# Attention's last reciprocals behind the projection's first split, its first tile by blocks of channels, and late ranks in layer 1

## The chip, the cores and the metric

The kernel runs on one core of a Trainium2 chip. The metric is device microseconds (us) of one execution. The kernel before takes 2798.72 us, the median of three runs (2797.06 to 2804.81).

## The reference

Two layers of a diffusion transformer block over 1024 latent tokens and 256 context tokens, 1024 channels wide. In each layer the normed tokens go through one input projection into four mixers of 256 channels each (a gated linear recurrence, a chunked gated recurrence, a state-space scan and latent attention with four heads); their outputs are concatenated, projected, gated and added, and an expert layer follows in which each of 16 experts picks its tokens.

```
h = modulate(rmsnorm(x, norm1_w[l]), mod_l[0], mod_l[1])
...
p = softmax(scores); y_m = p @ v                      # attention: latents see context and latents
x = x + mod_l[2] * (concatenate([ya, yb, ys, ym]) @ w_out[l])
h = modulate(rmsnorm(x, norm2_w[l]), mod_l[3], mod_l[4])
x = x + mod_l[5] * expert_choice_ffn(h, moe_router[l], ...)
# the context goes the same way in layer 0; layer 1 drops it after the mixers
```

The change concerns the end of attention (`ym`) and the start of `concatenate(...) @ w_out`.

## The kernel before, in words

Work is written as generators ("threads": `mla` for attention, `lw` for w_out, `wout` and `woutc` for the projection of latents and context, `route`, `exp` and others), each with a rank in `ORDER`, a low number first. `weave` (line 230) takes the ready thread of the lowest rank, lets it emit instructions up to its next `yield`, and advances a planner's clock. A `yield "s"` leaves a thread ready at once, a yield of a number makes it wait that long on the planner's clock, `wait` and `room` yield False until a flag is set or a pool of buffers has room. What comes out is an order by priority; a compiler's scheduler then fills each engine's queue from it, by priority among what it takes to be ready, and each engine works through its queue in that order. `issue_after(ins)` tells that scheduler that an instruction stands behind `ins` on its engine.

Products in float32 are made of three float32r products: every operand is split into a high half (copied by ScalarE) and a low half (subtracted by VectorE) (`split`, line 537); a "block" of one channel group is three matmuls of 128x512.

Attention (`attend`, line 1440) works on a pair of heads and two halves of 512 latents. For each of ten groups of keys it makes scores (three matmuls for each of four combinations of half and head), exponentials on ScalarE (into C tiles E in the first pass, M tiles in the others), products with the values, and running sums of the exponentials in E. At the end a matmul with ones gives the sums, VectorE takes their reciprocal and multiplies. Pair 0's result is stored in the DRAM tensor yT (line 1484); pair 1's stays in SBUF as y7, high and low.

`load_wout` (line 1498) loads w_out in eight pieces of 128 channels, splits them, and sets the flags `w{l}.0` to `w{l}.7`; pieces 0 to 4 may be split when pair 0's scores are done, 5 to 7 when pair 1's are, for they take over attention's buffers (tag A). `wout` (line 1525) goes over tiles of 128 tokens: two for the context (layer 0 only, first) and eight for the latents. A tile is loaded from yT (line 1542) and split; its two halves of 512 output channels take eight blocks of three matmuls each; VectorE gates and adds, ScalarE squares, VectorE norms and modulates, POOL adds, and TensorE transposes the tile for the router. The context's tiles have all eight channel groups in yT; the latents' take groups 0 to 6 from yT and group 7 from y7. The next tile's loads and split are emitted one tile ahead, in the first tile only behind its last block (`load(1)`). In layer 1 `wout` starts at rank 2.5, and goes back to rank 30 when its first loads are emitted.

Of the kernel before, what the change touches and what calls it, by code (L numbers as in the profile page):

```python
# [9 lines left out]
F32 = mybir.dt.float32  # L10
# [11 lines left out]
D = 1024  # L22
# [18 lines left out]
    dict(derived=0.5, ada0=-2, ada=20, norm=-3, eproj=1, lru0=6.01, lru1=8.078, gate0=3.4, gate1=7.01, ssd=3.43, z=6.95,  # L41
         g=7, v=0.079, hgrn0=6.614, hgrn1=6.757, group0=1.91, group1=3.41, hout0=6.767, hout1=3.44, chunk=6.713, prep=1.5,
         mla=6.757, max=3.4, lw=3.41, wout=30, route=31, woutc=29, routec=31.5, exp=33, al=0.74, be=0.25, be_g=0.14,
         be_hgrn0=1.01, be_lw=1.45, al_hout1=1.15, be_chunk=0.09, al_eproj=0.65, al_max=1.21, al_lru0=0.43, al_g=0.92,
         be_lru0=1.2, al_group1=0.69, be_hout0=1.85, al_hgrn0=1.12, be_gate1=0.49, be_mla=0.48, **{
# [120 lines left out]
class Model:  # L166
# [51 lines left out]
    def wait(self, *names):  # L218
        while not all(n in self.done for n in names):
            yield False  # L220

    def rank(self, name, p):
        for th in self.threads:
            if th[4] == name:
                th[0] = p

    def spawn(self, l, key, g, more=0.0):
        self.threads.append([self.order[l][key] + more, len(self.threads), 0.0, g, f"{key}{l}", key, None])
# [308 lines left out]
    def split(self, w, tag, tag2=None):  # L537

        nc = self.nc
        hi = self.t(tag, list(w.shape), F32R)  # L540
        lo = self.t(tag2 or tag, list(w.shape), F32R)
        nc.scalar.activation(hi, w, AF.Copy)
        nc.vector.tensor_sub(lo, w, hi.bitcast(F32))
        return hi, lo

    def proj_ch(self, l, c0, evac, groups=GROUPS):
# [769 lines left out]
    def mla(self, l, need):  # L1316
        nc = self.nc
        c, idx, _, _ = self.cols[l]
        c0 = 0 if need else 2
        SCALE = 96.0 ** -0.5  # L1320
        yield from self.wait(f"prep{l}")
        while self.left[l]:
            yield False
        vd = self.vd
        qs = self.t("qs", [128, 1])
        nc.vector.memset(qs, SCALE)
        nc.vector.scalar_tensor_tensor(qs[0:64], c[0:64, idx["qn"]:idx["qn"] + 1], SCALE,
                                       c[0:64, idx["kn"]:idx["kn"] + 1], op0=ALU.mult, op1=ALU.mult)

        HI = [self.t("A", [128, 2, 2, NT], F32R) for _ in range(2)]  # L1330
        LO = [self.t("A", [128, 2, 2, NT], F32R) for _ in range(2)]
        onef = self.ones[96:97, 0:1]
        for i in range(2):
            nc.gpsimd.memset(LO[i][96:97].rearrange("p a h t -> p (a h t)").bitcast(F32), 0.0)
            nc.scalar.activation(HI[i][96:97, 1].rearrange("p h t -> p (h t)"), onef.to_broadcast([1, 2 * NT]), AF.Copy)
        lat = [(256, 512), (768, 512)]
        runs = [(pr, [(0, 256)], 2) for pr in range(2) if need] + [(pr, lat, CH) for pr in range(2)]

        def maxima():
            for i, (pr, parts, ns) in enumerate(runs):  # L1340
                yield from self.att_max(l, HI[pr], parts, ns)
                self.done.add(f"max{l}.{i}")
        self.spawn(l, "max", maxima())
        X = {}

        def load(t, q):
            X[t, q] = self.t("M", [128, 4, 96])
            nc.sync.dma_start(X[t, q].rearrange("p h e -> p (h e)"), self.qkd[q, 128 * t:128 * t + 128, :])

        def place(t, q):  # L1350
            x = X.pop((t, q))
            T = slice(128 * t, 128 * t + 128)
            pk = self.p([128, 4, 128])
            for h in range(4):
                nc.tensor.transpose(pk[0:96, h, :], x[:, h, :], self.ident)
            for i in range(2):
                ph = pk[0:96, 2 * i:2 * i + 2]
                hi, lo = HI[i][0:96, 1 - q, :, T], LO[i][0:96, 1 - q, :, T]
                if q:
                    nc.scalar.activation(hi, ph, AF.Copy, scale=qs[0:96])  # L1360
                    nc.vector.scalar_tensor_tensor(lo, ph, qs[0:96], hi.bitcast(F32), op0=ALU.mult, op1=ALU.subtract)
                else:
                    nc.scalar.activation(hi, ph, AF.Copy)
                    nc.vector.tensor_sub(lo, ph, hi.bitcast(F32))
        todo = [(t, 0) for t in range(CH)] + [(t, 1) for t in range(c0, CH)]
        for x in todo[:2]:
            load(*x)
        yield 3.0
        for i, x in enumerate(todo):
            if i + 2 < len(todo):  # L1370
                load(*todo[i + 2])
            place(*x)
            self.done.add(f"qk{l}.{x[0]}.{x[1]}")
            yield 0.0
        yield from self.room(4)
        V = [self.t("C", [128, CH // 2, 256]) for _ in range(2)]
        for i in range(2):
            nc.sync.dma_start(V[i], vd[640 * i:640 * i + 640, :].rearrange("(c p) e -> p c e", p=128))
        for i, (pr, parts, ns) in enumerate(runs):
            yield from self.wait(f"max{l}.{i}")  # L1380
            keep = None
            if ns == CH and pr == 1:
                yield from self.room(2)
                keep = self.y7 = [self.t("C", [128, NL], F32R) for _ in range(2)]
            yield from self.attend(HI[pr], LO[pr], V, pr, parts, ns, keep, f"att{l}.{pr}" if ns == CH else f"attc{l}.{pr}")
            if ns == CH:
                self.done.add(f"pair{l}.{pr}")
        self.free(4)
# [48 lines left out]
                nc.scalar.activation(HI[96:97, 0, hh, t0:t0 + n], pr_[96:97, :n], AF.Copy)  # L1437
            yield True

    def attend(self, HI, LO, V, pr, parts, ns, keep, flag):  # L1440
        nc = self.nc
        py = [self.p() for _ in parts]
        E = [self.t("C", [128, 2, 512]) for _ in parts]
# [29 lines left out]
            yield "s"  # L1473
        self.done.add(flag)

        for pi, (t0, n) in enumerate(parts):
            ps = self.p()
            for hh in range(2):
                nc.tensor.matmul(ps[64 * hh:64 * hh + 64, :n], self.ones[:, 0:64], E[pi][:, hh, :n], start=True, stop=True)
            o = self.t("M", [128, 512])  # L1480
            nc.vector.reciprocal(o[:, :n], ps[:, :n])
            nc.vector.tensor_mul(o[:, :n], o[:, :n], py[pi][:, :n])
            if keep is None:
                nc.scalar.dma_start(self.yT[768 + 128 * pr:896 + 128 * pr, t0:t0 + n], o[:, :n])
            else:
                hi, lo = [y[:, t0 - NC_:t0 - NC_ + n] for y in keep]
                nc.scalar.activation(hi, o[:, :n], AF.Copy)
                nc.vector.tensor_sub(lo, o[:, :n], hi.bitcast(F32))
            yield "s"
        yield "s"  # L1490

    def bcast_mod(self, l, s, j, tag="C"):

# [31 lines left out]
    def wout(self, l, s, base, h2d, logits):  # L1525
# [20 lines left out]
            Y[j] = hl, x  # L1546

        load(0)
        G = self.bcast_mod(l, s, 2)
        self.rank(f"wout{'c' if s else ''}{l}", 29 if s else 30)  # L1550
        yield 4.0

        def body(j):
# [1 line left out]
            xm = X[j] = self.t("W", [128, D])  # L1555
            ss = self.t("s1", [128, 2])
            pms = [self.p() for _ in range(2)]
            todo = [(hf, k) for hf in range(2) for k in range(own)] + [(hf, k) for hf in range(2) for k in range(own, 8)]
            if j:
                todo.sort()  # L1560
            for hf, k in todo:
                c = slice(512 * hf, 512 * hf + 512)
                pm = pms[hf]
                if True:
                    if k < own:
                        yh, yl = [y[:, k, :] for y in hl]
                    else:
                        yield from self.wait(f"pair{l}.1")
                        yh, yl = [y[:, 128 * j:128 * j + 128] for y in self.y7]
                    yield from self.wait(f"w{l}.{k}")  # L1570
                    w, wl = self.whi[k], self.wlo[k]
                    for pas, (y, w) in enumerate(((yh, w), (yl, w), (yh, wl))):
                        nc.tensor.matmul(pm, y, w[:, c], start=(k == 0 and pas == 0), stop=(k == 7 and pas == 2))
                    if k in (2, 4, 6):
                        yield "s"
                if k < 7:
                    continue
                if hf and j == 0:
                    yield from self.room(4)
                    n2 = self.t("C", [128, D])  # L1580
                    nc.sync.dma_start(n2, a["norm2_w"][l:l + 1].to_broadcast([128, D]))
                    A2 = self.bcast_mod(l, s, 4)
                    nc.vector.scalar_tensor_tensor(A2, A2, 1.0, n2, op0=ALU.add, op1=ALU.mult)
                    B2 = self.bcast_mod(l, s, 3)
                    mods.extend((A2, B2))
                    load(1)
                nc.vector.tensor_mul(xm[:, c], pm, G[:, c])
                nc.vector.tensor_add(x[:, c], x[:, c], xm[:, c])
                nc.scalar.activation(xm[:, c], x[:, c], AF.Square, accum_out=ss[:, hf:hf + 1])
# [496 lines left out]
    def layer(self, l):  # L2086
# [14 lines left out]
        if "o" in self.which:  # L2101
# [7 lines left out]
            if need:  # L2109
                lgc = self.t("lgc", [128, 2, 16])  # L2110
                self.spawn(l, "woutc", self.wout(l, 1, basec, h2c, lgc))
                self.spawn(l, "routec", self.route(l, 1, lgc, 2, 32))
            if not need:

                self.rank(f"wout{l}", 2.5)
            self.spawn(l, "exp", self.experts(l, need, base, basec, h2d, h2c))
        self.weave(l)
        if "o" in self.which:
# [54 lines left out]
```

## Time and profile before

| | |
|---|---|
| median of three runs | 2798.72 us |
| profiled execution | 2805.27 us, span 2803.2 us |
| TensorE matmul / weight load | 2422.1 us (86%) / 1847.7 us (66%) |
| VectorE / ScalarE / POOL | 1837.3 us (66%) / 1179.8 us (42%) / 766.5 us (27%) |
| share of the chain that ended last | PE 18%, DVE 7% are the largest |

The span is the time from the first to the last instruction of one profiled execution, and the share of an engine is its busy time in it. An engine's idle time is given in brackets in the timeline, with what ended it. Line 162 is a helper through which all computing instructions go, so instructions are told apart by the tags of their tiles (A, C, W, M; ps is PSUM, cf the identity, wr the router, sT the modulation's vector).

### The profile page before, as it was taken

The numbers are of one execution on the slowest core, as the hardware profiler recorded it, in microseconds if no ns is written. First come the engines' busy times: TensorE is split into PE (matmuls) and PEld (weight loads), VectorE is DVE, ScalarE is ACT, GpSimd is POOL, SyncE is SP. The second block draws the span as 40 slices with busy tenths as digits, with TensorE's granted clock in tenths as the row PEclk, the third lists the DMA queues.
The fourth block names the chain that finished last, engine by engine and source line by source line (L and its number), as shares of the span: only waits on it lengthen the run. The fifth ranks groups of instructions, "written<-read, shape, count | busy, mean of one in ns | idle before, by whom it ended". The sixth has DMA issues, their size and how long they took to land. (4 is left out here: it accounts for less than half of the span.)

```text
span 2803.2 us, 49815 instructions
## 1 busy us (share of the span) xinstructions
PE 2422.1 (86%) x19212; PEld 1847.7 (66%) x19212; DVE 1837.3 (66%) x3678; ACT 1179.8 (42%) x2010; POOL 766.5 (27%) x858
## 2 busy tenths in 40 slices
PE   6979999988898893999999699799969988669998
PEld 3758888544555672777677678688745546557776
DVE  5445475566786556776777746754778754589995
ACT  3345223234344222555555352522353342246664
POOL 0112231242531113112111012422444311234443
PEclk8989999999999896999999899899969998779999
DMA  6222235468212433788787411133331023469996
GB/s 254 63 68 66 61 93 183 138 224 293 75 52 97 161 133 129 263 278 284 259 304 262 149 40 43 55 100 103 95 118 40 19 102 132 165 235 385 381 371 224
DMA packets 243436, 455.40 MB, mean 162 GB/s; under 512 B 25688, under 2 KB 155096, under 8 KB 242176
## 3 DMA queue, kind: packets, MB, share of 16 engines
q1 hardware_dynamic: 190176, 365.75, 37.2%
q0 software_dynamic: 12096, 37.75, 5.7%
q10 hardware_dynamic: 40928, 48.72, 4.9%
q8 instruction: 151, 2.47, 0.4%
q14 instruction: 85, 0.70, 0.1%
HBM read 377.55 MB, written 74.60 MB: 161 GB/s over the span
## 5 line engine op out<-in xcount | busy, mean ns | idle before, releaser
L162 PE MATMUL ps<-A,W 128*128 128x512 f32 (+3 forms) x4160 | 964.1, 379 | 25.6 <-ACT W L162 22.7
L162 PEld LDWEIGHTS ps<-A,W 128*128 128x128 f32 x4160 | 739.1, 195 | 170.3 <-ACT W L162 25.7
L162 DVE TENSOR_TENSOR A<-C,A 128x1024 fp32r<-128x1024 f32 x342 | 425.3, 1279 | 114.0 <-ACT A L162 108.5
L162 ACT ACTIVATE M<-ps 128x512 f32<-128x512 f32 (+6 forms) x576 | 262.2, 468 | 511.5 <-PE ps L162 430.0
L162 ACT ACTIVATE A<-C 128x1024 fp32r<-128x1024 f32 x384 | 390.6, 1058 | 152.9 <-DMA C<-in_moe_w_down_dram 77.8
L162 PE MATMUL ps<-A,M 128*128 128x512 f32 x768 | 191.6, 404 | 10.4 <-ACT M L162 5.8
L162 PE MATMUL ps<-W,A 128*128 128x256 f32 x1344 | 189.2, 296 | 1.2 <-issue 0.8
L162 DVE TENSOR_TENSOR C<-C,M 128x512 f32<-128x512 f32 (+2 forms) x236 | 154.8, 671 | 41.4 <-ACT M L162 39.9
L162 PEld LDWEIGHTS ps<-A,M 128*128 128x128 f32 x768 | 146.0, 194 | 50.0 <-DVE M L162 10.5
L162 PEld LDWEIGHTS ps<-W,A 128*128 128x128 f32 x1344 | 173.7, 199 | 2.6 <-ACT M L162 0.5
L162 POOL TENSOR_TENSOR A<-C,A 128x1024 fp32r<-128x1024 f32 x42 | 124.3, 2967 | 150.2 <-ACT A L162 150.1
L162 ACT ACTIVATE W<-ps 128x512 fp32r<-128x512 f32 (+2 forms) x156 | 66.5, 477 | 197.0 <-PE ps L162 196.7
L162 PE MATMUL ps<-cf,M 128*128 128x128 f32 (+3 forms) x416 | 72.7, 303 | 88.5 <-DVE M L162 53.8
L162 PE MATMUL ps<-C,A 128*32 128x128 f32 (+1 forms) x2528 | 147.5, 290 | 0.0
L162 PE MATMUL ps<-A 96*128 96x512 f32 (+3 forms) x368 | 133.9, 420 | 9.8 <-ACT M L162 3.4
L162 PEld LDWEIGHTS ps<-C,A 128*32 128x32 f32 (+1 forms) x2528 | 134.6, 127 | 10.7 <-issue 5.6
L162 PE MATMUL ps<-A,C 128*128 128x512 f32 x352 | 135.2, 415 | 5.6 <-DVE C L162 5.6
L162 PEld LDWEIGHTS ps<-cf,M 128*128 128x128 f32 (+2 forms) x416 | 54.5, 153 | 115.3 <-issue 42.4
L162 ACT ACTIVATE C<-ps 128x512 f32<-128x512 f32 (+4 forms) x116 | 53.4, 468 | 179.1 <-PE ps L162 166.6
L162 POOL TENSOR_TENSOR W<-W,C 128x512 f32<-128x512 f32 x33 | 49.2, 1505 | 258.5 <-DVE W L162 166.3
L162 POOL DMA_INDIRECT dr<-W,it x16 | 25.3, 1579 | 339.2 <-DVE W L162 339.2
L162 DVE TENSOR_REDUCE mp<-ps 128x1 f32<-128x512 f32 (+1 forms) x200 | 109.9, 585 | 10.0 <-PE ps L162 9.6
(244 smaller groups left out, 3809.5 us busy)
## 6 DMA issues: line engine op xcount, KB each, us to landing
C<-in_moe_w_gate_dram SPq DMA_DIRECT2D x128, 512.0 KB, 6.6
C<-in_moe_w_up_dram SPq DMA_DIRECT2D x128, 512.0 KB, 4.8
C<-in_moe_w_down_dram SPq DMA_DIRECT2D x128, 512.0 KB, 7.5
W<-in_ada_w_dram SPq DMA_DIRECT2D x80, 512.0 KB, 4.6
W<-in_w_in_dram SPq DMA_DIRECT2D x40, 512.0 KB, 3.6
C<-dr SPq DMA_DIRECT2D x29, 512.0 KB, 4.2
dr<-M ACTq DMA_DIRECT2D x114, 128.0 KB, 2.3
M<-dr SPq DMA_DIRECT2D x46, 256.0 KB, 4.7
```

The costliest lines, as they stand in the source:

```text
L162: return f(*args, **kw)
```

## The change

Four edits. (1) In the last pair, the sums' matmuls are emitted for both halves first; then `attend` waits for the projection's first load and split to be emitted (`wl{l}`) and for w_out's last piece (`w{l}.7`), and only then come reciprocal, multiply and the split of y7, which move to `att_out`: the first reciprocal is queued behind the low half of the projection's first tile, the second behind the low half of y7's first part. (2) The first tile of the projection goes block by block, both halves of a channel group behind each other, as pieces of w_out become ready; the last group's two blocks come at the end. (3) The loads and the split of tile 1 come ahead of these last two blocks, and ahead of the loads of the norm weight and the two modulation rows. (4) In layer 1 the rank of `lw` goes from 3.41 to 8.49, behind attention's 6.757, and `wout` has rank 30 throughout; the method `rank` is gone.

```diff
@@ ORDER, layer 1
-         mla=6.757, max=3.4, lw=3.41, wout=30, ...
+         mla=6.757, max=3.4, lw=8.49, wout=30, ...
@@ split
-        nc.vector.tensor_sub(lo, w, hi.bitcast(F32))
+        self.low = nc.vector.tensor_sub(lo, w, hi.bitcast(F32)).ins
@@ attend, behind the passes over the keys
+        S = []
         for pi, (t0, n) in enumerate(parts):
             ps = self.p()
             for hh in range(2):
                 nc.tensor.matmul(ps[64 * hh:64 * hh + 64, :n], self.ones[:, 0:64], E[pi][:, hh, :n], start=True, stop=True)
-            o = self.t("M", [128, 512])
-            nc.vector.reciprocal(o[:, :n], ps[:, :n])
-            nc.vector.tensor_mul(o[:, :n], o[:, :n], py[pi][:, :n])
-            ...
+            S.append(ps)
+            if keep is None:
+                self.att_out(S, py, pr, parts, pi, None, None)
             yield "s"
+        if keep is not None:
+            yield from self.wait(f"wl{l}", f"w{l}.7")
+            last = self.first_low
+            for pi in range(len(parts)):
+                last = self.att_out(S, py, pr, parts, pi, keep, last)
         yield "s"
+    def att_out(self, S, py, pr, parts, pi, keep, last):
+        t0, n = parts[pi]
+        o = self.t("M", [128, 512])
+        with self.tc.issue_after(last) if last is not None else ExitStack():
+            nc.vector.reciprocal(o[:, :n], S[pi][:, :n])
+        nc.vector.tensor_mul(o[:, :n], o[:, :n], py[pi][:, :n])
+        if keep is None:
+            nc.scalar.dma_start(self.yT[768 + 128 * pr:896 + 128 * pr, t0:t0 + n], o[:, :n])
+            return None
+        hi, lo = [y[:, t0 - NC_:t0 - NC_ + n] for y in keep]
+        nc.scalar.activation(hi, o[:, :n], AF.Copy)
+        return nc.vector.tensor_sub(lo, o[:, :n], hi.bitcast(F32)).ins
@@ wout
         load(0)
+        self.first_low = self.low
         G = self.bcast_mod(l, s, 2)
-        self.rank(f"wout{'c' if s else ''}{l}", 29 if s else 30)
+        self.done.add(f"wl{l}")
         yield 4.0
@@ body(j)
+            if j == 0:
+                for k in range(7):
+                    yield from self.wait(f"w{l}.{k}")
+                    for hf in range(2):
+                        block(k, hf)
+                    yield "s"
+                yield from self.wait(f"w{l}.7", *([] if s else [f"pair{l}.1"]))
+                yield from self.room(4)
+                load(1)
+                n2 = self.t("C", [128, D])
+                ...
+            for hf in range(2):
+                for k in range(7 if j == 0 else 0, 8):
+                    block(k, hf)
+                    if k in (2, 4, 6):
+                        yield "s"
@@ layer
-            if not need:
-                self.rank(f"wout{l}", 2.5)
```

## Rows read from the trace of the kernel before

**Rows 1.** Windows: start:end length, busy of PE, PEld, DVE, ACT, POOL, clock, DMA.

```profile
840.00:890.00 50.00, 50.00 (x210) 27.36 (x208) 32.95 (x36) 27.09 (x44) 12.55 (x9) 1.00 0.17 56
2238.00:2300.00 62.00, 52.96 (x208) 28.56 (x207) 34.70 (x38) 29.27 (x46) 11.88 (x9) 0.92 0.26 94
...
2300.00:2332.00 32.00, 26.19 (x100) 20.11 (x99) 20.86 (x27) 5.08 (x10) 3.33 (x2) 0.84 0.39 123
```

**Rows 2.** Timeline of PE, layer 0: start, length, what, [idle before and its end].

```profile
890.04 1.92 PE L162 MATMUL ps<-W,sT 128*32 128x512 f32 x16
899.49 1.22 PE L162 MATMUL ps<-A,W 128*128 128x512 f32 x2 [7.53 <-ACT W L162]
...
916.18 0.50 PE L162 MATMUL ps<-A,C 128*128 128x512 f32 x1 [1.45 <-DVE C L162]
...
926.90 1.03 PE L162 MATMUL ps<-cf,W 128*128 128x128 f32 x8
```

**Rows 3.** Timelines of ACT, DVE and SP, layer 0, the end of attention.

```profile
897.27 1.22 ACT L162 ACTIVATE C<-M 128x512 fp32r<-128x512 f32 x2 [9.00 <-DVE M L162]
898.40 1.04 ACT L162 ACTIVATE W<-C 128x1024 fp32r<-128x1024 f32 x1
...
886.42 3.80 DVE L162 TENSOR_TENSOR A<-W,A 128x1024 fp32r<-128x1024 f32 x3 [0.94 <-ACT A L162]
890.14 6.56 DVE L162 RECIPROCAL M<-ps 128x512 f32<-128x512 f32 x2
896.62 1.21 DVE L162 TENSOR_TENSOR M<-M,ps 128x512 f32<-128x512 f32 x2
...
855.82 0.43 SPq L1542 DMA_DIRECT2D C<-dr  x1
```

**Rows 4.** Timeline of PE, the second pair's start in layer 0 and in layer 1.

```profile
840.25 0.50 PE L162 MATMUL ps<-A 97*128 97x512 f32 x1
...
2237.81 0.51 PE L162 MATMUL ps<-A 97*128 97x512 f32 x1
...
2253.21 4.16 PE L162 MATMUL ps<-C,C 128*64 128x512 f32 x8 [7.60 <-ACT C L162]
```

**Rows 5.** Timelines of ACT and SP, layer 1, the second pair's start.

```profile
2241.58 0.60 ACT L162 ACTIVATE M<-ps 128x512 f32<-128x512 f32 x1 [5.53 <-PE ps L162]
...
2251.72 0.95 ACT L162 ACTIVATE W<-C 128x896 fp32r<-128x896 f32 x1 [4.43 <-DMA C<-dr]
2252.58 2.04 ACT L162 ACTIVATE C<-ps 128x512 f32<-128x512 f32 x4
...
2247.79 0.36 SPq L1542 DMA_DIRECT2D C<-dr  x1
```

**Rows 6.** Timelines of PE, ACT, DVE and SP, layer 1, the first two latent tiles.

```profile
2300.31 0.51 PE L162 MATMUL ps<-A,W 128*128 128x512 f32 x1
...
2310.14 1.56 PE L162 MATMUL ps<-A,C 128*128 128x512 f32 x6
2315.29 1.22 PE L162 MATMUL ps<-A,W 128*128 128x512 f32 x2 [3.59 <-ACT W L162]
2318.73 0.79 PE L162 MATMUL ps<-A,C 128*128 128x512 f32 x1 [2.22 <-DVE C L162]
...
2331.85 1.03 PE L162 MATMUL ps<-cf,W 128*128 128x128 f32 x8
...
2314.30 0.93 ACT L162 ACTIVATE W<-C 128x896 fp32r<-128x896 f32 x1
...
2300.40 6.55 DVE L162 RECIPROCAL M<-ps 128x512 f32<-128x512 f32 x2
...
2299.59 0.37 SPq L1542 DMA_DIRECT2D C<-dr  x1
```

**Rows 7.** Timeline of PE, layer 0, last context tile and first latent tiles.

```profile
935.39 1.97 PE L162 MATMUL ps<-cf,W 128*128 128x128 f32 x8 [4.70 <-POOL W L162]
...
954.09 0.50 PE L162 MATMUL ps<-A,C 128*128 128x512 f32 x1 [1.93 <-DVE C L162]
```

More of the change, by code (lines that the diff above doesn't have):

```diff
@@ L42 @@
          g=7, v=0.079, hgrn0=6.614, hgrn1=6.757, group0=1.91, group1=3.41, hout0=6.767, hout1=3.44, chunk=6.713, prep=1.5,
-         mla=6.757, max=3.4, lw=3.41, wout=30, route=31, woutc=29, routec=31.5, exp=33, al=0.74, be=0.25, be_g=0.14,
+         mla=6.757, max=3.4, lw=8.49, wout=30, route=31, woutc=29, routec=31.5, exp=33, al=0.74, be=0.25, be_g=0.14,
          be_hgrn0=1.01, be_lw=1.45, al_hout1=1.15, be_chunk=0.09, al_eproj=0.65, al_max=1.21, al_lru0=0.43, al_g=0.92,
@@ L220, in wait @@
             yield False
[L222 to L225, printed above, removed]
     def spawn(self, l, key, g, more=0.0):
@@ L1384, in mla @@
                 keep = self.y7 = [self.t("C", [128, NL], F32R) for _ in range(2)]
-            yield from self.attend(HI[pr], LO[pr], V, pr, parts, ns, keep, f"att{l}.{pr}" if ns == CH else f"attc{l}.{pr}")
+            yield from self.attend(l, HI[pr], LO[pr], V, pr, parts, ns, keep, f"att{l}.{pr}" if ns == CH else f"attc{l}.{pr}")
             if ns == CH:
@@ L1438, in att_max, with attend @@
             yield True
-    def attend(self, HI, LO, V, pr, parts, ns, keep, flag):
+    def attend(self, l, HI, LO, V, pr, parts, ns, keep, flag):
         nc = self.nc
@@ L1479, in attend @@
                 nc.tensor.matmul(ps[64 * hh:64 * hh + 64, :n], self.ones[:, 0:64], E[pi][:, hh, :n], start=True, stop=True)
-            o = self.t("M", [128, 512])
-            nc.vector.reciprocal(o[:, :n], ps[:, :n])
-            nc.vector.tensor_mul(o[:, :n], o[:, :n], py[pi][:, :n])
+            S.append(ps)
             if keep is None:
[L1484 to L1488, printed above, removed]
-            yield "s"
-        yield "s"
+                self.att_out(S, py, pr, parts, pi, None, None)
+            yield "s"
+        if keep is not None:
[3 more added lines that the diff above has]
+                last = self.att_out(S, py, pr, parts, pi, keep, last)
+        yield "s"
+    def att_out(self, S, py, pr, parts, pi, keep, last):
+        nc = self.nc
+        t0, n = parts[pi]
[9 more added lines that the diff above has]
+        return nc.vector.tensor_sub(lo, o[:, :n], hi.bitcast(F32)).ins
     def bcast_mod(self, l, s, j, tag="C"):
@@ L1557, in body, with block @@
             pms = [self.p() for _ in range(2)]
[L1558 to L1561, printed above, removed]
+            def block(k, hf):
+                c = slice(512 * hf, 512 * hf + 512)
+                if k < own:
+                    yh, yl = [y[:, k, :] for y in hl]
+                else:
+                    yh, yl = [y[:, 128 * j:128 * j + 128] for y in self.y7]
+                w, wl = self.whi[k], self.wlo[k]
+                for pas, (y, w) in enumerate(((yh, w), (yl, w), (yh, wl))):
+                    nc.tensor.matmul(pms[hf], y, w[:, c], start=(k == 0 and pas == 0), stop=(k == 7 and pas == 2))
@@ new lines, in body @@
+            if j == 0:
[8 more added lines that the diff above has]
+                n2 = self.t("C", [128, D])
+                nc.sync.dma_start(n2, a["norm2_w"][l:l + 1].to_broadcast([128, D]))
+                A2 = self.bcast_mod(l, s, 4)
+                B2 = self.bcast_mod(l, s, 3)
+                mods.extend((A2, B2))
@@ L1562, in body @@
+            for hf in range(2):
                 c = slice(512 * hf, 512 * hf + 512)
                 pm = pms[hf]
[L1564 to L1573, printed above, removed]
+                for k in range(7 if j == 0 else 0, 8):
+                    block(k, hf)
@@ L1574, in body @@
                     if k in (2, 4, 6):
                         yield "s"
-                if k < 7:
-                    continue
                 if hf and j == 0:
[L1579 to L1582, printed above, removed]
                     nc.vector.scalar_tensor_tensor(A2, A2, 1.0, n2, op0=ALU.add, op1=ALU.mult)
-                    B2 = self.bcast_mod(l, s, 3)
-                    mods.extend((A2, B2))
-                    load(1)
```

## The prediction

> **What bounds the kernel now.** Read the table of the page first: TensorE is busy for most of the span, so a microsecond is worth something where TensorE stands still and nowhere else. Then the windows of the stretches that the diff touches [rows 1]. The second head pair of the latents' attention is the same work in both layers; in layer 0 TensorE is busy through all of 840 to 890 at a granted clock of 1.00, in layer 1 the stretch is 12 us longer, with 9 us idle and a clock of 0.92. The start of the output projection in layer 1 (2300:2332) idles 5.8 us at 0.84. Last, the timeline of TensorE for the gaps, and those of ScalarE (ACT), VectorE (DVE) and SyncE (SP) for what ended them. There are four places.
>
> **A, layer 0, first context tiles** [rows 2, 3]. Attention ends at 890.0, 16 matmuls of the modulation run to 892.0, then TensorE idles 7.53 us for ACT's copy (high half) of the first tile, at 898.40. Its data was asked for at 855.82. In between VectorE does three low halves of w_out, two reciprocals (6.56) and y7; ACT sits 9.00 us waiting to copy y7, and the copy of the tile stands behind that. So 6.56 us of reciprocals stand in front of 2.3 us of splitting (1.04 the copy, a third of 3.80 the low half). A later gap of 1.45 waits for tile 1's low half.
>
> **B, layer 0, first latent tile**: 1.93 us for tile 1's low half [rows 7].
>
> **C, layer 1, start of the second pair** [rows 4, 5]. From its first scores (2237.81) to the projection's first matmul [rows 6] are 62.5 us; in layer 0, 840.25 to 890.04, 49.8. The 12.7 are a gap of 7.60, shorter waits ahead of it, and matmuls at half clock behind it (eight of them took 4.16). TensorE waits for the first pass's exponentials at 2252.58, and these stand on ACT behind the split of the projection's first tile (2251.72), which itself waited 4.43 us for a load issued at 2247.79. The second pass's exponential ran already at 2241.58: the first pass's were placed late, after the split that rank 2.5 puts ahead of them.
>
> **D, layer 1, first latent tile** [rows 6]. Its matmuls start without a gap and reach attention's channels at 2310.14, so the reciprocals (2300.40, 6.55) are hidden here. Then 3.59 for ACT's copy of tile 1 (2314.30, behind tile 0's work on ACT, though its load went out at 2299.59) and 2.22 for its low half; what follows is partly at half clock.
>
> **The change, part by part.** A matmul of the projection takes 0.234 us at full clock: 42 of them from 2300.31 to 2310.14 [rows 6]; a tile has 48, so 11.2 us, two tiles 22.5.
>
> *Reciprocals behind the first split, A.* ACT's copy can follow the third w_out copy, the low half the third low half (886.42 + 3.80 = 890.2), so it ends at 891.5, when the modulation's 16 matmuls end (892.0). From 890.04 to the transposes at 926.90 are 36.9 us; without gaps 22.5 + 2.9 (24 modulation matmuls at 1.92/16) = 25.4. That gains 11.5. Queued behind the moved reciprocals on VectorE are y7, which only the latents need, after 935 [rows 7], and tile 1's low half. Two rounds of reciprocal, multiply, wait for ACT's copy and subtract are 2 x (3.3 + 0.6 + 0.6 + 0.6) = 10.2 [rows 3], so VectorE is free at 901.7 and that low half there at 903; TensorE wants it at about 904. PSUM: two banks of output, two of sums, two of tile 0 and one of modulation are 7 of 8; the next tile needs two, and the first reciprocal frees one at 895. If this cover fails, the 1.45 stays: I take 10.0. Bounds: -2 (the order bends round the longer hold of the banks) to 11.5.
>
> *First tile by blocks, tile 1's loads earlier, A, B and D.* The number of matmuls is unchanged. Half 0 no longer evacuates beside half 1: two multiplies (1.2) on VectorE after the tile, beside tile 1's 11.2 on TensorE. Tile 1's two loads pass three loads on SP (norm weight, two modulation rows) that are needed only after tile 0 ends. ACT's copy of tile 1 then precedes tile 0's work on ACT. B gains 1.9, or 0 if VectorE still comes late. D: from 2300.31 to 2331.85 are 31.5, without gaps 22.5, so 9.0. The low half now sits among the reciprocals and y7 (10.2 us after 2300.40), which may cost up to 1.2: I take 7.9; the bounds are 0, if the new gap is as long, and 9.0. Attention's last channels are wanted 9.8 us after the tile's start; y7's first half is ready some 5.1 us after the reciprocals begin, as it no longer waits for the second reciprocal: no cost.
>
> *Late ranks in layer 1, C.* With rank 30, load and split come after the pair's instructions in the program, as in layer 0, where the pair runs without a gap: 12.7 at most. Five w_out copies (1.0 on ACT) and low halves (1.3 on VectorE) lose their rank as well; in layer 0's pair ACT is busy 27 of 50 us and VectorE 33 [rows 1], so there is room. But the load still can't go out before pair 0's results are stored, at about 2247.8, and its copy ran at 2251.72. By the row, a copy holds ACT until its data is there: four exponentials stood behind it [rows 5]. If it stands behind the second pass's exponentials (which would end at 2237.81 + 24 x 0.234 + 0.6 = 2244.0 without today's order), the third pass's wait until 2252.7. TensorE has its next products in hand to about 2251.6 (2243.4, two times 2.0 for the eight matmuls of rows 4 at full clock, and 18 x 0.234), and with the catching up loses some 2.5. I take 10.2; bounds 0 and 12.7. The Trainium skill has this as a rule (TensorE: Matmul & The Clock Gate, section "Architectural detail: the array is 16× 32×32, not 1× 128×128"): ScalarE and VectorE are strict first in, first out, and only TensorE's queue reorders, by pulling weight loads ahead. By it the place in ACT's queue sets the price and not the rank, so the sum has the 2.5; if ACT could pass by a waiting copy, the sum would be 2.5 higher. The trace agrees (4.43 us of ACT idle in front of four ready exponentials).
>
> Sum: 10.0 + 1.9 + 10.2 + 7.9 = 30.0, of at most 35.1. All four places lie in a serial part: what follows (the other tiles, routing, experts) starts when the tiles before are done, and is moved, not shortened. The profiled execution took 2805.27 (span 2803.2 and 2.1 around it), so 2775.3 on its scale; it lies 6.5 above the median 2798.72, on whose scale it is 2768.7: **2769 us**.
>
> **Rivals.**
> 1. *C's gap has another cause* (pair 0's reciprocals hold PSUM banks, or its stores hold ACT; the waits ahead of the gap speak for that). Against: layer 0 has the same reciprocals and stores and no gap. C gains 0: 2798.7 - 19.8 = 2779.
> 2. *The change doesn't do what it says in layer 0*: the split needs a W buffer, and these are held by w_out pieces and modulation weights until 890 to 892. For: modulation weights wait in them for TensorE. Against: the third low half, which frees one, ends at 890.2. A gains 0: 2779.
> 3. *A stall takes the place*: the evacuation chain becomes the bound. Ahead of the last context tile's transposes TensorE waits 4.70 for POOL [rows 7]; the same wait after each of the first tiles of A, B and D is 14.1: 2783. Against: tile 1's 11.2 us lie between.
> 4. *Slower: ACT's queue in layer 1.* All eight w_out copies and the tile's now fall somewhere into the second pair, and the loads behind the tile's are held on SP to 2247.8. Each copy that stands in ACT's queue ahead of its data and of a pass's exponentials can cost what today's one costs, 12.7. With n such waits the time is 2798.7 - 35.1 + 12.7 n: two are 2789, three bring it level, four are slower: 2814. For: five of the eight loads are still to be issued then. Against: layer 0's copies ran in the pair's gaps, and the pair took 49.8.
>
> **How the numbers follow.** The forecast 0.62 (its own range 2760 to 2777), rival 1 0.12, rival 2 0.11, rival 3 0.08, rival 4 with two or three waits 0.04, with four 0.03. The range takes in rivals 1 to 3 and two waits, up to 2789; down to the full 35.1 and 6 us more, for matmuls behind B's gap at half clock and for the spread of the runs shown: 2757. A measurement tells about 0.3% (8.4 us) from no change. Faster: the forecast, rivals 1 to 3 less what goes wrong beside them, 0.89; within: two or three waits and what I have not thought of, 0.06; slower: four waits and as much for an order that goes wrong elsewhere, 0.05.
>
> **What would show it.** A: the gap ahead of the first context tile under 2 us, and the reciprocals behind the tile's low half. C: 50 to 53 us from the pair's first scores to the projection's first matmul, exponentials of the first pass before those of the second. D: no gap over 1.5 us between the first two latent tiles, and a clock near 1.00 there. B: the 1.93 gone. From the last tile on, the two traces should run in parallel. Wrong would be a pair of over 58 us, a first context tile still behind y7's copies, or a stretch after the tiles that is over 5 us longer than now.

## The result, and the profile after

The changed kernel takes 2764.66 us (median, 2762.82 to 2768.59) beside 2797.89 (2795.55 to 2804.81) for the kernel before: a ratio of 0.9864, 95% interval 0.9844 to 0.9885. The forecast was 2769 us, a gain of 30.0 of at most 35.1; the measured gain is 33.2. The kernel before, measured anew beside the experiments, took 2801 to 2808 us, so kernels are compared by their ratio to the kernel before of the same round, not by their times.

The windows of the changed kernel, the same stretches as [rows 1] and the first tiles' (columns: window, length, busy time of PE, PEld, DVE, ACT and POOL with counts, granted clock, DMA share, GB/s):

```profile
843.00:893.00 50.00, 50.00 (x213) 27.36 (x212) 32.95 (x36) 27.99 (x45) 12.53 (x9) 1.00 0.18 57
2226.00:2277.00 51.00, 51.00 (x213) 28.00 (x212) 37.40 (x39) 29.15 (x46) 11.86 (x9) 1.00 0.30 108
...
2276.00:2297.00 21.00, 21.00 (x92) 16.87 (x91) 19.04 (x27) 4.41 (x8) 2.28 (x2) 1.00 0.49 151
```

The second pair now runs alike in both layers, and the first latent tiles of layer 1 have no idle time, both at a granted clock of 1.00 (before, in layer 1: 0.92 and 0.84).

Place A, timeline of TensorE, then ACT and DVE [rows 2, 3]:

```profile
892.98 1.92 PE L162 MATMUL ps<-W,sT 128*32 128x512 f32 x16
894.84 0.50 PE L162 MATMUL ps<-A,W 128*128 128x512 f32 x1
...
900.58 1.89 PE L162 MATMUL ps<-W,sT 128*32 128x512 f32 x8
...
919.21 1.03 PE L162 MATMUL ps<-cf,W 128*128 128x128 f32 x8
...
891.12 1.04 ACT L162 ACTIVATE W<-C 128x1024 fp32r<-128x1024 f32 x1
898.32 0.63 ACT L162 ACTIVATE C<-M 128x512 fp32r<-128x512 f32 x1 [6.15 <-DVE M L162]
904.77 1.06 ACT L162 ACTIVATE W<-C 128x1024 fp32r<-128x1024 f32 x1 [5.82 <-DMA C<-dr]
...
893.08 1.21 DVE L162 TENSOR_TENSOR C<-C,W 128x1024 fp32r<-128x1024 f32 x1
894.22 3.35 DVE L162 RECIPROCAL M<-ps 128x512 f32<-128x512 f32 x1
...
899.59 3.35 DVE L162 RECIPROCAL M<-ps 128x512 f32<-128x512 f32 x1
...
905.87 1.23 DVE L162 TENSOR_TENSOR C<-C,W 128x1024 fp32r<-128x1024 f32 x1 [1.79 <-ACT W L162]
```

Copy and low half come ahead of the reciprocals, and the first tile starts on the heels of the modulation, without a gap. From the modulation's start to the transposes are 26.2 us (36.9 before).

Places C and D, layer 1 [rows 4 to 6]: TensorE, ACT, DVE and SP.

```profile
2226.36 0.50 PE L162 MATMUL ps<-A 97*128 97x512 f32 x1
...
2276.20 0.51 PE L162 MATMUL ps<-A,W 128*128 128x512 f32 x1
...
2287.41 0.39 PE L162 MATMUL ps<-A,W 128*128 128x512 f32 x1
...
2298.57 1.04 PE L162 MATMUL ps<-cf,W 128*128 128x128 f32 x8
...
2227.38 2.68 ACT L162 ACTIVATE C<-ps 128x512 f32<-128x512 f32 x4 [2.76 <-PE ps L162]
2230.14 2.64 ACT L162 ACTIVATE M<-ps 128x512 f32<-128x512 f32 x4
...
2234.95 1.29 ACT L162 ACTIVATE M<-ps 128x512 f32<-128x512 f32 x2 [2.18 <-PE ps L162]
2236.40 1.23 ACT L162 ACTIVATE M<-ps 128x512 f32<-128x512 f32 x2 [0.15 <-PE ps L162]
2239.86 0.60 ACT L162 ACTIVATE M<-ps 128x512 f32<-128x512 f32 x1 [2.24 <-PE ps L162]
2240.36 0.94 ACT L162 ACTIVATE W<-C 128x896 fp32r<-128x896 f32 x1
...
2280.94 0.94 ACT L162 ACTIVATE W<-C 128x896 fp32r<-128x896 f32 x1
...
2285.73 1.08 DVE L162 TENSOR_TENSOR C<-C,W 128x896 fp32r<-128x896 f32 x1
...
2234.85 0.36 SPq L1553 DMA_DIRECT2D C<-dr  x1
```

The first pass's exponentials stand ahead of the second's, and the split's copy (2240.36) waits for nothing. The pair takes 49.84 us, the first latent tiles 22.37 from first matmul to transposes (31.54 before); tile 1's low half ends at 2286.8, 0.6 us before that tile's first matmul (2287.41).

All kernels side by side, in us, from the timelines of TensorE. A: from the last of the attention's sums in layer 0 to the first context tile's transposes. B: from the last context tile's transposes to the first latent tile's. C: between the last sums of layer 1's two pairs. D: from those to the first latent tile's transposes. "Tiles": from the last sums to the last tile's transposes, the whole stage in each layer. e8 moves the transposes into the next tile, so A, B and D do not compare there. The places are read from one profiled execution of each kernel.

| kernel | A | B | tiles, layer 0 | C | D | tiles, layer 1 | ratio to before (interval) |
|---|---|---|---|---|---|---|---|
| before | 37.4 | 31.0 | 178.9 | 62.5 | 32.1 | 132.6 | 1 |
| changed | 26.8 | 27.0 | 166.5 | 49.8 | 22.9 | 121.3 | 0.9864 (0.9844 to 0.9885) |
| e1 ranks back | 25.9 | 25.9 | 163.6 | 62.6 | 22.8 | 122.7 | 0.9907 (0.9877 to 0.9937) |
| e2 ranks only | 37.3 | 31.0 | 178.8 | 49.8 | 39.3 | 139.7 | 0.9965 (0.9947 to 0.9982) |
| e3 reciprocals back | 35.5 | 26.2 | 173.3 | 49.8 | 33.2 | 131.7 | 0.9923 (0.9899 to 0.9947) |
| e4 loads late | 29.8 | 31.2 | 171.1 | 49.8 | 27.6 | 127.8 | 0.9882 (0.9859 to 0.9906) |
| e5 half by half | 25.9 | 26.1 | 160.8 | 49.8 | 22.9 | 121.3 | one run, 2769.30 us |
| e6 no order on DVE | 27.6 | 27.7 | 166.9 | 49.8 | 24.5 | 122.7 | one run, 2769.97 us |
| e7 load's rank back | 25.9 | 27.3 | 163.5 | 49.8 | 22.9 | 121.3 | one run, 2756.51 us |
| e8 router inside | | | 146.5 | 49.8 | | 114.2 | 0.9802 (0.9779 to 0.9825) |
| e9 projection's rank back | 26.0 | 26.5 | 164.4 | 49.8 | 22.9 | 121.3 | 0.9865 (0.9843 to 0.9886) |
| e10 first tile as before | 30.0 | 31.1 | 171.3 | 49.8 | 27.6 | 127.8 | 0.9906 (0.9885 to 0.9928) |

Changed against before: 12.3 + 12.7 + 11.3 = 36.3 us in the places. The two profiled executions lie 42.4 us apart, as the one of the kernel before was above its median. The rest lies where nothing was changed: ahead of the last sums of layer 0 (889.5 us before, 892.5 changed), from layer 0's last tile to the last sums of layer 1's first pair (1168.9 and 1166.9) and behind the last transposes of layer 1 (370.8 and 363.8). These stretches vary from 889 to 900, from 1160 to 1171 and from 362 to 371 us over the profiles of the other kernels with the same code there (e1 to e7, e9, e10), so they say nothing of the change. The tiles vary too: in layer 0, e1, e7 and e9, whose edits lie in layer 1, take 163.5 to 164.4 us where the changed kernel takes 166.5.

### The profile page after: what moved, and what is told of

The parts are those of the page before. It is cut to its first block, busy times and chain, and to the rows that moved or that the text cites. A ratio compares the mean times of both kernels' runs of the same rounds, so it can differ in the third digit from the quotient of the medians.

```text
span 2760.8 us, 49818 instructions
## 1 busy us (share of the span) xinstructions
PE 2408.9 (87%) x19212; PEld 1839.7 (67%) x19212; DVE 1833.4 (66%) x3678; ACT 1186.9 (43%) x2010; POOL 769.9 (28%) x858
## 5 line engine op out<-in xcount | busy, mean ns | idle before, releaser
L162 PEld LDWEIGHTS ps<-A,W 128*128 128x128 f32 x4160 | 734.6, 194 | 159.8 <-issue 20.8
L162 DVE TENSOR_TENSOR A<-C,A 128x1024 fp32r<-128x1024 f32 x342 | 419.3, 1257 | 123.5 <-ACT A L162 115.6
L162 ACT ACTIVATE A<-C 128x1024 fp32r<-128x1024 f32 x384 | 398.0, 1059 | 182.1 <-DMA C<-in_moe_w_down_dram 66.8
L162 DVE TENSOR_TENSOR C<-C,M 128x512 f32<-128x512 f32 (+2 forms) x236 | 156.4, 679 | 35.5 <-ACT M L162 34.0
L162 POOL TENSOR_TENSOR A<-C,A 128x1024 fp32r<-128x1024 f32 x42 | 117.0, 2792 | 152.9 <-ACT A L162 133.5
L162 PE MATMUL ps<-cf,W 128*128 128x128 f32 (+1 forms) x536 | 86.5, 301 | 37.0 <-POOL W L162 16.4
```

Source lines behind the costliest of these rows:

```text
L162: return f(*args, **kw)
```

## The experiments

The theory on record adds up four places, each with its own cause. The rival to it, once the traces were compared, is that the parts lean on each other.

**e1: both ranks of layer 1 back.**

```
-mla=6.757, max=3.4, lw=8.49, wout=30
+mla=6.757, max=3.4, lw=3.41, wout=30
+if not need: self.rank(f"wout{l}", 2.5)      # and back to 30 once load(0) is issued
```

> The changed kernel with the two ranks of layer 1 set back (load of w_out at 3.41, projection raised to 2.5); all else as changed. Theory (C's gap comes from these ranks alone, and from nothing else of the change): the pair's stretch in layer 1, from its first scores to the projection's first matmul, goes from 49.8 back to about 62.5 us, with a gap of about 7.6 ended by ACT ahead of the first pass's products; A, B and D stay as changed; the time is 2764.7 + 12.7 = 2777 us (2774 to 2780). Rival 1 of the prediction (C's gap has another cause, and its going is a side effect of the moved reciprocals or of the early loads): the stretch stays at about 50 us and the time at 2765.

C is back, alone, at 62.6 us, and the ratio of 0.9907 is 12 us above that of the changed kernel. TensorE and ACT:

```profile
2233.27 3.67 PE L162 MATMUL ps<-C,C 128*64 128x512 f32 x7 [7.71 <-ACT C L162]
...
2231.78 0.95 ACT L162 ACTIVATE W<-C 128x896 fp32r<-128x896 f32 x1 [4.16 <-DMA C<-dr]
2232.64 2.04 ACT L162 ACTIVATE C<-ps 128x512 f32<-128x512 f32 x4
```

It is the picture of [rows 4, 5]: a copy whose load has not landed, four exponentials behind it, TensorE idle for them. Rival 1 falls.

**e7 and e9: one rank at a time.** Of e1's edit, e7 has the first line, e9 the second.

```
-lw=8.49, wout=30
+lw=3.41, wout=30                             # e7
+if not need: self.rank(f"wout{l}", 2.5)      # e9
```

> The changed kernel with one of the two ranks of layer 1 set back: the load of w_out at 3.41, the projection left at 30. Theory: what hurt was the projection's first split ahead of the first pass's exponentials, and that takes the projection's own early rank as well; the pair's stretch stays at 49.8 us. Rival: the early load of w_out alone brings the w_out copies and the split forward, and the stretch is back at 62.5.

> The changed kernel with the other one of the two ranks of layer 1 set back: the projection raised to 2.5, the load of w_out left at 8.49. Theory (either rank alone is harmless: the projection waits for the first split piece of w_out, so a late load holds it back whatever its own rank): the pair's stretch stays at 49.8 us, and the time at that of the changed kernel, 0.986 of the kernel before. Rival (the projection's rank alone puts its split ahead of the first pass's exponentials): 62.5 us in the stretch, 0.991.

Both hold 49.8. e9 is at 0.9865, the ratio of the changed kernel once more; e7 was run once. Either rank set late is enough; it takes both ranks early to lose the 12.7 us.

**e2: late ranks alone, in the kernel before.**

> The kernel before with the late ranks of layer 1 alone. Theory 'additive' (the sum of the prediction: each place is its own): C's 12.7 us go and D's 9.2 stay, 2797.9 - 12.7 = 2785 us. Theory 'leaning' (with late ranks the first tile's split comes after the attention's last work in the program, so without the move of the reciprocals it stands behind them in layer 1 as it did in layer 0 before): the pair's stretch shortens by 12.7, but a gap like A's (7.5 us before the first tile's matmuls, 10.6 with the half clock behind it) appears in layer 1 after the pair: 2797.9 - 12.7 + 7.5 to 10.6 = 2793 to 2796 us, that is, hardly any gain.

C goes (49.8), and 7.2 of it come back in D (39.3). TensorE, ACT, DVE and SP at the end of layer 1's attention:

```profile
2292.33 1.22 PE L162 MATMUL ps<-A,W 128*128 128x512 f32 x2 [8.47 <-ACT W L162]
...
2309.44 1.04 PE L162 MATMUL ps<-A,W 128*128 128x512 f32 x2 [3.88 <-ACT W L162]
...
2290.22 1.22 ACT L162 ACTIVATE C<-M 128x512 fp32r<-128x512 f32 x2 [11.03 <-DVE M L162]
2291.35 0.93 ACT L162 ACTIVATE W<-C 128x896 fp32r<-128x896 f32 x1
...
2283.07 6.57 DVE L162 RECIPROCAL M<-ps 128x512 f32<-128x512 f32 x2 [3.85 <-PE ps L162]
...
2242.44 0.36 SPq L1542 DMA_DIRECT2D C<-dr  x1
```

The tile's data was asked for at 2242.44; its copy runs 49 us later, because y7's two copies stand ahead of it on ACT and wait 11.03 us for the reciprocals. Loads of this kind (448 KB) took 3.6 us to land in the median there. That is A's stall of [rows 3], moved into layer 1, and it is what 'leaning' said. The net gain is 5.5 us by the trace. The runs alone would not have shown this: their ratio of 0.9965 is 9.8 us, with an interval from 5.0 to 14.8 that holds the 12.7 of 'additive' and lies just above the 2 to 5 of 'leaning'. The Trainium skill's rule on queues (TensorE: Matmul & The Clock Gate, section "Architectural detail: the array is 16× 32×32, not 1× 128×128": ScalarE and VectorE are strict first in, first out) agrees with these rows: a copy that had its data passed nothing.

**e3: the reciprocals at their old place, the rest as changed.**

```
-            S.append(ps)
-            if keep is None:
-                self.att_out(S, py, pr, parts, pi, None, None)
+            self.att_out(S, py, pr, parts, pi, keep, None)
...
-            yield from self.wait(f"wl{l}", f"w{l}.7")
```

> The changed kernel with the last pair's reciprocals at their old place (inline after the sums, with no wait for the split and no order behind its low half); ranks, blocks and early loads as changed. Theory 'additive': only A returns in layer 0 (26.2 us from the sums' end to the first context tile's transposes become 36 to 37), layer 1 is as changed, as its reciprocals were hidden before: 2764.7 + 10.6 = 2775 us. Theory 'leaning': layer 1 gets a gap of the same kind, as its split is no longer early in the program: 2764.7 + 10.6 + 7.5 to 10.6 = 2783 to 2786 us. If the early load of the second tile was what helped in A, the time stays near 2765.

Again the parts lean: A is 8.7 us longer than in the changed kernel, and D, which 'additive' left as it was, 10.3 longer. The ratio of 0.9923 is 16.5 us above that of the changed kernel; with the intervals of both this fits either theory (10.6, or 18 to 21), so it is the gap in layer 1 that decides. TensorE in layer 0 and layer 1:

```profile
899.49 1.22 PE L162 MATMUL ps<-A,W 128*128 128x512 f32 x2 [7.54 <-ACT W L162]
...
2281.94 1.22 PE L162 MATMUL ps<-A,W 128*128 128x512 f32 x2 [8.48 <-ACT W L162]
```

**e6: the reciprocals behind the split in the program, without the explicit order on VectorE.**

```
-        with self.tc.issue_after(last) if last is not None else ExitStack():
-            nc.vector.reciprocal(o[:, :n], S[pi][:, :n])
+        nc.vector.reciprocal(o[:, :n], S[pi][:, :n])
```

> The changed kernel without the explicit order of the two reciprocals behind a low half; they still come after the first split in the program. Theory: the place in the program is enough for the first tile, the second reciprocal then follows the first directly and the low half of the second tile comes some 3.3 us later: A between 26.8 and 28.2 us (the gap of 1.45 of before), D between 22.9 and 25. Rival: the explicit order is what counts, the reciprocals run first, as they are ready when the sums are: A 33 us or more, since the low half waits 6.6 us.

The place in the program does most of it: A and D are 27.6 and 24.5. VectorE keeps the first low half in front and then does both reciprocals in one go. But TensorE gets back the 1.45 of [rows 2], and in layer 1 the 1.2 that the prediction had as D's possible loss. DVE and ACT in layer 0, then TensorE in both layers:

```profile
893.95 1.21 DVE L162 TENSOR_TENSOR C<-C,W 128x1024 fp32r<-128x1024 f32 x1
895.09 6.55 DVE L162 RECIPROCAL M<-ps 128x512 f32<-128x512 f32 x2
...
907.60 1.39 DVE L162 TENSOR_TENSOR W<-ps,C 128x512 f32<-128x512 f32 x2 [3.02 <-PE ps L162]
908.90 2.42 DVE L162 TENSOR_TENSOR C<-C,W 128x1024 fp32r<-128x1024 f32 x3
...
904.57 1.06 ACT L162 ACTIVATE W<-C 128x1024 fp32r<-128x1024 f32 x1 [1.12 <-DMA C<-dr]
...
910.17 0.50 PE L162 MATMUL ps<-A,C 128*128 128x512 f32 x1 [1.46 <-DVE C L162]
...
2290.69 0.50 PE L162 MATMUL ps<-A,C 128*128 128x512 f32 x1 [1.31 <-DVE C L162]
```

The reciprocals are over by then and are not what the low half waits for. Tile 1's copy is done at 905.63, but VectorE stands idle for 3.02 us, because tile 0's two multiplies come first (907.60) and wait for TensorE; the low half follows at 908.90. With the explicit order it starts at 905.87, behind both reciprocals and ahead of those multiplies. So what the explicit order changes is what stands ahead of tile 1's low half on VectorE.

**e4: the second tile's loads behind the first tile's last matmul.** In the program they then stand behind half 0's evacuation (multiply, add and square of its output) and ahead of half 1's.

```
-                yield from self.room(4)
-                load(1)
-                n2 = self.t("C", [128, D])            # and A2, B2
...
                 if hf and j == 0:
+                    yield from self.room(4)
+                    n2 = self.t("C", [128, D])        # and A2, B2
+                    load(1)
                     nc.vector.scalar_tensor_tensor(A2, A2, 1.0, n2, op0=ALU.add, op1=ALU.mult)
```

> The changed kernel with the second tile's loads, and the three loads for the norm and the modulation rows ahead of them, back behind the first tile's last matmul; reciprocals, ranks and blocks as changed. Theory: D returns (gaps of about 3.6 and 2.2 us between the first two latent tiles of layer 1, 9.2 us with the half clock), the same pair of waits appears in layer 0 between the two context tiles and again between the first two latent tiles (before: 1.45 and 1.93, where half 0's evacuation ran beside half 1; now both halves end together, so up to 5.8 each): 2764.7 + 9.2 + 3.4 to 11.6 = 2777 to 2785 us, nearer the lower. Rival (the block order or the moved evacuation, not the loads, removed D's gaps): under 3 us slower.

A is 3.1 us longer than in the changed kernel, B 4.1 and D 4.7, which is half of D only. The ratio of 0.9882 is 5 us above that of the changed kernel, within the noise of the two; the trace has 11.1 us in the two tile stages. In layer 0 the gap of 1.93 of [rows 7] is back. One gap is in D:

```profile
2294.49 0.50 PE L162 MATMUL ps<-A,C 128*128 128x512 f32 x1 [2.90 <-DVE C L162]
```

**e10: the whole first tile as before** (half by half, half 0 evacuated first, then the loads), to find the other half of D. In the context's tile half 0 is evacuated ahead of the whole second half. In the latents' tile it is evacuated behind the seven channels of both halves, where it stands in e4, in the changed kernel and in the kernel before; there e10 differs from e4 mainly by the order of the blocks.

```
-            if j == 0:
-                for k in range(7): ...                # both halves of a channel, then load(1)
+            todo = [(hf, k) for hf in range(2) for k in range(own)] + [(hf, k) for hf in range(2) for k in range(own, 8)]
+            for hf, k in todo: ...                    # block(k, hf); at k == 7 evacuate; n2, A2, B2, load(1) at hf == 1
```

> The changed kernel with the whole first tile as before: half by half, half 0 evacuated ahead of the second half's channel 7, and only then the second tile's loads; reciprocals behind the split and late ranks as changed. With the loads merely behind the last matmul, but ahead of both evacuations, D had 27.6 us, 4.5 short of the kernel before. Theory (ScalarE's copy of the second tile stands behind half 0's square): D is back at about 32 us from the sums to the first latent tile's transposes, with two gaps of about 3.6 (ended by ACT) and 2.2 (ended by DVE); A at 27 to 30; about 0.991 of the kernel before. Rival (the 4.5 came from the reciprocals and y7 by turns, which free VectorE sooner): D stays at 27.6 and the ratio at 0.988.

My theory failed: D is 27.6 as in e4, with the same single gap. The ratio of 0.9906 is the one that the theory gave, but it can't be told from e4's 0.9882, and the places are e4's to 0.2 us:

```profile
2293.73 0.50 PE L162 MATMUL ps<-A,C 128*128 128x512 f32 x1 [2.90 <-DVE C L162]
```

So the block order does not carry the other 4.5 us of D. What is left of the change in e10 is the moved reciprocals and the late ranks. With the ranks back (e1) D stays at 22.8, which speaks for the reciprocals; but e1 has the early loads too, and no run moves the reciprocals alone, so this half is argued and not shown. One difference can be read from the two timelines, and no run isolates it: ACT's copy of tile 1 runs at 2289.11 in e10, ahead of tile 0's squares (2292.11), and in the kernel before behind them (2314.30, [rows 6]).

**e5: half by half over the first seven channels, loads early.**

```
-                for k in range(7):
-                    for hf in range(2):
+                for hf in range(2):
+                    for k in range(7):
```

> The changed kernel with the first tile's first seven channels half by half, as before (channel 7 last for both halves, loads early, reciprocals behind the split). Theory: the block order is worth nothing by itself, as the w_out pieces are split before the tile starts (their third low half ends 0.9 us before the first low half begins): A stays at 26.8 us from the sums to the first context tile's transposes, D at 22.9 from the sums to the first latent tile's. Rival (the order lets the tile start on pieces that come late): A or D over 1 us longer.

A is 25.9 and D 22.9, as in e7 and e9: the order of the blocks is worth nothing.

**e8: the router's steps inside the next tile.** What remained idle in the changed kernel's tile stages pointed to a further version:

```
                     block(k, hf)
+                    if lg is not None and hf and k in (3, 5, 7):
+                        next(lg, None)
...
-                yield from body(j)
-            if j:
-                if j == nt:
-                    yield 5.0
+                yield from body(j, logit(j - 1) if j else None)
+            else:
+                yield 14.0 if s else 5.0
                 yield from logit(j - 1)
```

> The changed kernel with each tile's router steps (transposes, router products, selection) put among the second half's matmuls of the next tile, behind channels 3, 5 and 7, instead of behind its last one; the last context tile's go into the first latent tile. What remains idle in the changed kernel's tile stages (919 to 1059 and 2298 to 2397) is 15.7 and 12.7 us, mostly 1.18 ahead of each selection, one 4.70, and matmuls at half clock behind them (granted 0.91 and 0.95). Theory (these waits are only order): all but the last tile's go, and the clock returns: 12 to 25 us, 2764.7 - 20 = 2745 us, or 0.979 of the kernel before (0.977 to 0.983). Rival (the chain from a tile's last matmul to its transposes, 8.5 us in the wait for POOL ahead of the second context tile's, does not fit into the 8.4 us that then lie between): a wait for POOL of 1 to 3 us appears ahead of most transposes and the gain is under 8 us.

The ratio is 0.9802, within the 0.977 to 0.983 of the theory: e8 is faster than the kernel before and than the changed kernel, whose interval begins at 0.9844. Windows of the tile stages, the changed kernel first, then e8, and the longest wait ahead of a router step inside e8's tiles of layer 1:

```profile
919.20:1059.00 139.80, 118.99 (x636) 92.16 (x634) 77.48 (x198) 31.18 (x76) 25.36 (x18) 0.90 0.46 157
2298.60:2397.00 98.40, 85.73 (x472) 66.17 (x470) 49.34 (x117) 22.51 (x54) 19.69 (x13) 0.95 0.46 157
```

```profile
890.00:1038.00 148.00, 137.99 (x751) 102.68 (x747) 92.88 (x197) 37.45 (x87) 29.42 (x20) 0.98 0.56 190
2266.00:2380.00 114.00, 104.97 (x570) 81.26 (x566) 72.03 (x143) 27.14 (x62) 24.99 (x15) 0.99 0.50 167
```

```profile
2288.56 0.66 PE L162 MATMUL ps<-cf,W 128*128 128x128 f32 x4 [1.01 <-POOL W L162]
```

The first window shows 20.8 us idle (139.80 less 118.99), not the 15.7 of the expectation. The stages shorten by 20.0 and 7.1 us, and the clock is 0.98 and 0.99. The rival's wait for POOL is there, at about a microsecond in the first tiles, and does not decide. Of the 27 us some 17 arrive by the ratios: from layer 0's last tile to layer 1's first pair e8 takes 1178.2 us, above the 1160 to 1171 of the others. There ACT's waits for the experts' down weights, from the end of the tile stage to 1500, come to 72.5 us, against 59.8 in the changed kernel (in 462 us and 441). That would fit experts that start earlier and wait for their weights; but TensorE's own waits change there as well (for VectorE's M tiles from 18.4 to 36.6 us, for one load from 20.0 to 5.8), so the cause stays open.

## Why the prediction was right, and where not

**A.** Right in mechanism: the gap of 7.53 is gone and the reciprocals follow the low half. Forecast 10.0, measured 10.6, and 11.4 in e1, e5, e7 and e9, which keep the change in A (25.9 to 26.0): the bound of 11.5. The 1.45 that I left in the sum as a cover that might fail did not come; e6 shows what keeps it away. My working gave the early loads no part beyond that 1.45; e4 and e10 put 3.1 to 3.2 on them.

**B.** Right in cause: with the loads late again (e4, e10) the gap of 1.93 returns and the stretch is 31.1 to 31.2, with the reciprocals back instead (e3) it is 26.2. The term was mis-sized: 1.9 forecast, 4.0 measured in the stretch itself, since it counted the idle time alone. Behind the gap the granted clock was 0.63 from 954.1 to 958.0; in the changed kernel it is 1.00 from 937.0 to 954.7. The tiles behind it give 2.3 back in the changed kernel's profile, 1.7 net over layer 0; in e1, e7 and e9 the net is 3.1 to 3.9.

**C.** Right in cause, and the term was mis-sized: 12.7, not 10.2. The step that failed is "with the catching up loses some 2.5": I put the split's copy behind the second pass's exponentials, where it would hold the third pass. It stands at 2240.36, behind all four exponentials of the third pass and the first of the fourth; its load went out at 2234.85, and it waits for nothing. The sentence that rank 2.5 puts the split ahead tells half of it: e7 and e9 show that it took both ranks.

**D.** 7.9 forecast, 9.2 measured. Another 2.2 lie in the tiles behind it (132.6 to 121.3 are 11.3 in all), which I had at nothing; in e1, whose tiles are those of the changed kernel, they are 0.6, so they are not the change's for certain. The 1.2 for the low half did not come, again by the order that e6 lacks. The attribution was wrong: that the reciprocals "are hidden here" holds only while the split is early. Taken out of the changed kernel, the moved reciprocals cost 10.3 in D (e3) and the early loads 4.7 (e4); that the rest of the 9.2 is the reciprocals' alone is argued from e10. That half 0 "no longer evacuates beside half 1" holds for the context's tile only.

**The sum** gives each edit a place of its own, and that step failed, though the whole came out. The late ranks alone are worth 5.5 us by the trace and not 12.7 (e2), and the reciprocals' move, taken out of the finished change, costs 17.2 over the two tile stages and not A's 10.6 (e3: 173.3 and 131.7 against 166.5 and 121.3). The prediction saw nowhere that the late ranks put D's split behind the reciprocals. That the same change moves the reciprocals kept the sum whole, and as no reason was given for it, this was luck. With all parts in, each closes the stall that another would open, so the bounds, not the discounts, were the better estimate: 35.1 against 36.3 in the traces.

Rival 2 fell with A, rival 3 with B and D (the 4.70 ahead of the second context tile's transposes stays, but no new one appears), rival 4 with C: no copy waits in the pair.

## What to carry to other kernels

Where an engine takes its work in order, ask of every moved instruction what stands ahead of it at its new place: e2's copy had its data and still waited for work that no one needed yet. A stall's cost is not tied to the edit that removes it; before a sum of places is trusted, ask of each edit what it does with the others left out. Look also at the stage behind the one that was shortened: of e8's 27 us in the tiles some 17 arrived.

## What was not expected of the hardware

A stall cost more than its idle time. In e2 two gaps of 8.47 and 3.88 us stand in D, 12.4 together, and D is 16.4 us longer than in the changed kernel (39.3 against 22.9); in e3 one gap of 8.48 made it 10.3 longer. Behind each, matmuls run at half speed for a while: the two behind e2's gap of 8.47 took 1.22 us, where two take 0.63 in the changed kernel's tile. The granted clock (before the last two columns) is 0.50, the level of 1.2 GHz, behind that gap, and then 1.00, the level of 2.4 GHz:

```profile
2292.30:2296.00 3.70, 3.67 (x8) 2.56 (x9) 3.69 (x4) 3.70 (x5) 0.00 (x0) 0.50 0.00 0
2296.00:2305.00 9.00, 9.00 (x40) 7.29 (x40) 3.08 (x3) 1.02 (x2) 0.00 (x0) 1.00 0.05 7
```

Eight modulation matmuls inside the first context tile took 1.89 us in the changed kernel's profile, and 1.06 to 1.11 in those of the kernel before and of all experiments but e8, which splits them into two fours. A window on the start of the eight shows two begun together in the changed kernel, four in the kernel before:

```profile
900.58 0.62 PE L162 MATMUL ps<-W,sT 128*32 128x512 f32 x2
...
907.70 0.64 PE L162 MATMUL ps<-W,sT 128*32 128x512 f32 x4
```

That is the 0.8 by which A missed its bound; why only two start together there is not explained.
